# Where the norm, the scores and the inverse stand in the gaps of an RWKV-7 recurrence: a new order of the work beside the chain

## The chip, the core and the metric

The kernel runs on one core of a Trainium2 chip. A core has five engines that each work through a queue of their own, in its order: TensorE (PE in the profile; its weight loads are PEld), VectorE (DVE), ScalarE (ACT), GpSimd (POOL) and SyncE (SP), which here issues the transfers between the chip's memory and the core. An engine waits for another, or for a transfer, at a semaphore, and what stands behind the waiting instruction in its queue waits with it. The metric is the device time of one execution, in microseconds (us), as the median of several runs.

## What is computed

The reference is a decoder of two layers over 1040 tokens (16 meta tokens and 1024 of input) of width 1024, in float32: a layer of RWKV-7 time mixing, a layer of stick-breaking attention, each followed by a conv-gated MLP. The change lies in the time mixing. Cut to that part, with 16 heads of 64:

```python
kk = kk / jnp.maximum(jnp.linalg.norm(kk, axis=-1, keepdims=True), 1e-12)
decay = jnp.exp(-jnp.exp(heads(w_log)))
seq = tuple(jnp.moveaxis(t, 1, 0) for t in (rh, decay, kh, vh, -kk, kk * ah))
def step(S, inp):
    r_t, w_t, k_t, v_t, a_t, b_t = inp
    sa = jnp.einsum('bhij,bhj->bhi', S, a_t)
    S = (S * w_t[:, :, None, :] + sa[..., None] * b_t[:, :, None, :]
         + v_t[..., None] * k_t[:, :, None, :])
    return S, jnp.einsum('bhij,bhj->bhi', S, r_t)
_, y = lax.scan(step, S0, seq)
mu = jnp.mean(y, axis=-1, keepdims=True)
var = jnp.mean(jnp.square(y - mu), axis=-1, keepdims=True)
y = ((y - mu) * lax.rsqrt(var + GN_EPS)).reshape(bsz, L, C) * lnx_g + lnx_b
y = y + bonus                     # sum(r * k * r_k) * v
return (y * g) @ w_o
```

## The kernel before

The scan is done in chunks of 64 tokens (`rwkv_chain`). Within a chunk the steps become matrix products and the inverse of a triangular matrix; from chunk to chunk only the state S goes on. The first 16 tokens are a chunk of their own (`first_chunk`). The other 1024 tokens are two segments of 8 chunks, and the heads are four groups of four, so there are eight **units**, one for each segment and group, each with 8 chunks.

`stage_c` is the serial chain of a unit. For each chunk PE forms c1 (S against the scaled keys), DVE adds KV and writes R, PE forms c2 with the inverse XT, DVE and ACT copy the result into UV, PE forms c3 and the output yp, and DVE writes the next S. Three times in a chunk, behind c1, behind c2 and behind c3 and yp, it calls `gap()`, and there work for other units is put into the queues. A unit so has 24 gaps, gap 0 to gap 23; gaps 3k, 3k+1 and 3k+2 are those of chunk k.

What a gap gets stands in the table `SEQ`, one word for each gap, each letter one step of a generator. In unit i:

- A: a step of `stage_a` of unit i+2. It loads BK and AR (the load of AR goes into the tiles ARz), forms the scores between them on PE, masks them on DVE into Aa, and sends their diagonal blocks through memory into another layout (AD is written, AT is read back): the *lanes*. P is its first step, the load of BK, for unit i+3.
- S, s: a step of `stage_s`, the substitution that inverts the diagonal blocks, of unit i+2 (S) or i+1 (s). It copies XL from xinit on DVE, then does 62 tensor operations on POOL, a product into prd and a sum into XL in turn, each of which needs the one before. At the end XL is written to memory as XD. A unit's substitution is done partly under S, in the unit before, partly under s.
- x, X: a step of `stage_x` of unit i+1. The first (x) first runs what is left of that unit's substitution, and loads XD back as X11t. The second transposes X11t into X on DVE and copies it into XT on ACT (XTb in the trace). Six more finish the inverse on PE and ACT.
- B, V, T: masked scores against r (Ar), the turned v and its product KV, and the turned BK, all of unit i+1.
- F: a step of `stage_f` of unit i-1, the norm of its output y. Step 1 loads g into the tile GB. Step 2 squares y on ACT (ysq), multiplies y by g on POOL, and loads b into the same tile GB. Steps 3 and 4 are four products each on PE (hr_gn), 5 to 9 the reciprocal root on DVE and ACT, 10 and 11 two products each on PE (hp_gn) for one half of y. Step 12 multiplies this half on DVE and starts the other one, step 13 ends its products, and step 14 multiplies the second half on DVE, adds b to y on POOL and writes y out. In unit 0, F is the rest of `first_chunk`.

PE, DVE, POOL and SP keep the order in which the generators write (`InOrder`, `pmm`); on ACT the scheduler places most instructions. In the last unit, `beside` adds steps of the output projection from gap 13 on.

Of the kernel before, what the change touches and what calls it, by code (L numbers as in the profile page):

```python
# [51 lines left out]
def kernel(ctx: ExitStack, tc: tile.TileContext, a: dict, out: bass.AP):  # L52
# [729 lines left out]
    def rwkv_chain(late, early, last):  # L782
# [564 lines left out]
        def run(gs):  # L1347
# [8 lines left out]
        ).split()  # L1356
        NZ = (1, 4, 12)
        SEQ = (
            "ATsss TVsss TTsss AAsss AAsss AAsss AAsss Asss FBsss BBsss xFV BFV "
            "BFVS BFVSSS BFVSSS BFVSSS BFVSSS XVFSSS XFSSS XFSSS XFSSS XFSSS XFPSSS XFFSSSS "  # L1360
        ).split()

        def warm(n):
# [198 lines left out]
    def rest():  # L1562
# [300 lines left out]
        def chain_and_wo(es):  # L1863
# [40 lines left out]
            def last():  # L1904
# [9 lines left out]
                return work  # L1914

            run(rwkv_chain(*pools, last))
            late.close()
            rw.close()
# [620 lines left out]
```

## Time and profile before

| | us |
|---|---|
| median of 3 runs | 3629.34 (3625.01 to 3632.36) |
| the profiled execution | 3628.45 |
| its span, first to last instruction | 3626.7 |
| the eight units, first c1 to the end of the last chunk | 432.8 (754.85 to 1187.60) |
| mean granted clock of PE over the span, share of full | 0.911 |

The profile is one execution, and its times count from the first instruction. What lies outside the span is 1.75 us. The units are 12% of the span; the projections ahead of them and the second layer and MLPs behind them are not touched. The start of a unit is called U here, and U+10 is a point 10 us into it. In the timeline a row is start, duration, engine, line, operation and the tiles it writes and reads; the bracket at its end is the idle time of the engine before it, and what ended it. Several operations of one kind in a row are merged, and x4 counts them. The rows are further down, ahead of the prediction.

### The profile page before, as it was taken

The numbers are of one execution on the slowest core, as the hardware profiler recorded it, in microseconds if no ns is written. First come the engines' busy times: TensorE is split into PE (matmuls) and PEld (weight loads), VectorE is DVE, ScalarE is ACT, GpSimd is POOL, SyncE is SP. The second block draws the span as 40 slices with busy tenths as digits, with TensorE's granted clock in tenths as the row PEclk, the third lists the DMA queues.
The fourth block names the chain that finished last, engine by engine and source line by source line (L and its number), as shares of the span: only waits on it lengthen the run. The fifth ranks groups of instructions, "written<-read, shape, count | busy, mean of one in ns | idle before, by whom it ended". The sixth has DMA issues, their size and how long they took to land.

```text
span 3626.7 us, 62709 instructions
## 1 busy us (share of the span) xinstructions
PE 3120.0 (86%) x25101; PEld 2913.6 (80%) x25101; DVE 2329.0 (64%) x3128; ACT 1554.7 (43%) x2859; POOL 1735.9 (48%) x1678
## 2 busy tenths in 40 slices
PE   4798688567778979999899988888889699998998
PEld 4796466456667969999899978788878699998998
DVE  8778866523333588888733377777774988887342
ACT  4664545133335333333333266666654333334232
POOL 5555634344535564454422366666644544444231
PEclk7898799768777989999999999999999799999999
DMA  6344333433335422222445200110035222224453
GB/s 202 104 152 140 123 122 116 119 94 98 106 99 156 138 65 77 83 71 80 150 137 167 90 27 24 27 30 24 21 108 168 90 79 77 77 81 138 122 170 94
DMA packets 439454, 366.61 MB, mean 101 GB/s; under 512 B 66855, under 2 KB 359485, under 8 KB 438907
## 3 DMA queue, kind: packets, MB, share of 16 engines
q1 hardware_dynamic: 438299, 361.28, 33.0%
q8 instruction: 197, 3.23, 0.4%
q0 software_dynamic: 864, 1.33, 0.1%
q14 instruction: 94, 0.77, 0.1%
HBM read 266.51 MB, written 96.02 MB: 100 GB/s over the span
## 4 chain that ended last, share of the span: by engine, by line
PE 45%; DVE 20%; DMA 9%; ACT 6%; issue 5%; POOL 4%; SPq 2%; ACTq 0%; DVEq 0%; POOLq 0%
PE dn L1517 12%; DVE t L1700 5%; DVE om L2254 2%; PE kps L2099 2%; DVE rs L1625 2%; DMA AD<-Aa 2%; PE c L797 1%; POOL be L2257 1%; SPq L44 1%; ACT t L1698 1%; PE wt L2102 1%; PE kp L217 1%; DMA XD<-XL 1%; PE av L2099 1%; PE A L797 1%
## 5 line engine op out<-in xcount | busy, mean ns | idle before, releaser
L1517 PE MATMUL dn<-act,h_dn 128*128 128x260 f32 x2688 | 437.5, 284 | 4.8 <-ACT act L76 2.4
L1517 PEld LDWEIGHTS dn<-act,h_dn 128*128 128x128 f32 x2688 | 373.5, 190 | 5.8 <-ACT act L76 2.8
L1700 DVE SCALAR_TENSOR_TENSOR t<-u,pcol,t 128x1040 f32<-128x1040 f32 x168 | 303.4, 1806 | 108.9 <-ACT t L1698 108.9
L1517 PE MATMUL dn<-act,l_dn 128*128 128x260 f32 x1344 | 273.4, 285 | 1.7 <-POOL l_dn L1466 1.7
L2257 POOL TENSOR_TENSOR be<-be,om 128x911 f32<-128x911 f32 (+7 forms) x128 | 195.8, 1530 | 131.1 <-DVE om L2254 106.6
L1466 POOL TENSOR_TENSOR l_dn<-r_dn,h_dn 128x1024 fp32r<-128x1024 f32 (+1 forms) x46 | 102.5, 2228 | 323.5 <-ACT h_dn L76 322.8
L2254 DVE TENSOR_TENSOR_SCAN om<-om 128x912 f32<-128x912 f32 (+7 forms) x128 | 214.0, 1672 | 49.2 <-POOL om L2249 30.4
L1715 POOL TENSOR_TENSOR t<-t,t 128x1040 f32<-128x1040 f32 x42 | 102.5, 2440 | 253.4 <-DVE t L1700 253.4
L76 ACT ACTIVATE h_dn<-r_dn 128x1024 fp32r<-128x1024 f32 (+1 forms) x92 | 90.7, 986 | 298.2 <-PE dn L1517 276.7
L1517 PEld LDWEIGHTS dn<-act,l_dn 128*128 128x128 f32 x1344 | 207.3, 189 | 2.2 <-POOL l_dn L1466 2.2
L1466 POOL TENSOR_TENSOR s34l<-rs,s34h 128x1024 fp32r<-128x1024 f32 x44 | 105.8, 2404 | 101.1 <-ACT s34h L76 101.1
L76 ACT ACTIVATE WT<-wt 128x512 fp32r<-128x512 f32 (+2 forms) x224 | 98.8, 443 | 117.1 <-PE wt L2102 88.8
L797 PE MATMUL A<-ARz,BK 128*128 128x128 f32 x512 | 91.3, 326 | 58.9 <-DMA ARz<-AR_s 34.1
L2320 DVE TENSOR_TENSOR WT<-wt,WT 128x512 fp32r<-128x512 f32 (+2 forms) x224 | 107.6, 488 | 51.6 <-ACT WT L76 48.2
L2099 PE MATMUL av<-WT,VS 128*128 128x256 f32 (+3 forms) x640 | 108.7, 283 | 32.9 <-DVE WT L2320 32.7
L76 ACT ACTIVATE s34h<-rs 128x1024 fp32r<-128x1024 f32 x44 | 46.7, 1062 | 202.2 <-PE p110S L1652 5.0
L1466 DVE TENSOR_TENSOR l_dn<-r_dn,h_dn 128x1024 fp32r<-128x1024 f32 (+1 forms) x46 | 52.0, 1131 | 122.6 <-ACT h_dn L76 122.5
L2102 PE MATMUL wt<-ident,be 128*128 128x128 f32 x576 | 99.2, 295 | 33.6 <-DVE WTm L2295 33.5
L797 PEld LDWEIGHTS A<-ARz,BK 128*128 128x128 f32 x512 | 75.6, 224 | 65.2 <-issue 34.8
L217 PE MATMUL kp<-xm,wh_rw_wk 128*128 128x264 f32 (+1 forms) x384 | 109.0, 376 | 19.1 <-DVE xm L396 10.5
L2249 POOL TENSOR_SCALAR_AFFINE_SELECT be<-be 128x128 f32<-128x128 f32 x128 | 78.0, 610 | 90.0 <-ACT be L2244 90.0
L2099 PEld LDWEIGHTS av<-WT,VS 128*64 128x64 f32 (+1 forms) x640 | 85.5, 165 | 44.0 <-DVE WT L2320 42.9
(2105 smaller groups left out, 11090.1 us busy)
## 6 DMA issues: line engine op xcount, KB each, us to landing
r_dn<-in_ffn_down_dram SPq DMA_DIRECT2D x60, 512.0 KB
a_s<-t SPq DMA_DIRECT2D x84, 260.0 KB
rv<-in_ffn_up_dram SPq DMA_DIRECT2D x42, 512.0 KB
ra<-in_ffn_up_dram SPq DMA_DIRECT2D x42, 512.0 KB
araw<-a_s SPq DMA_DIRECT2D x50, 260.0 KB
r_dn<-in_ffn_down_dram SPq DMA_DIRECT2D x32, 384.0 KB
raw<-a_s SPq DMA_DIRECT2D x36, 260.0 KB
hr<-h_s SPq DMA_DIRECT2D x32, 260.0 KB
```

What stands on the lines that cost most here:

```text
L76: return S.activation(o, i, AF.Copy, scale=scale)
L217: return tc.keep_in_program_order(mm(*args, **kw))
L797: return tc.keep_in_program_order(mm(*args, **kw))
L1466: eng.tensor_tensor(lo, x, f(hi), op=ALU.subtract)
L1517: self.mm(ps[:, c, :], w[:, kk, :], X[k][i][:, c * CH : (c + 1) * CH], start=k == 0 and j == 0, stop=k == len(X) - 1 and j == 2,)
L1700: VV.scalar_tensor_tensor(t[j], u[j][:, i : i + n], w, t[j], op0=ALU.mult, op1=ALU.add)
L1715: (G if n == L else VV).tensor_tensor(t[1], t[0], t[1], op=ALU.mult)
L2099: return tc.keep_in_program_order(mm(*args, **kw))
L2102: return tc.keep_in_program_order(nc.tensor.transpose(*args))
L2254: V.tensor_tensor_scan(om[0:nq, 0:nk], om[0:nq, 0:nk], om[0:nq, 0:nk], 1.0, op0=ALU.mult, op1=ALU.min)
L2257: G.tensor_tensor(be[0:nq, 1:nk], be[0:nq, 1:nk], om[0:nq, 0 : nk - 1], op=ALU.mult)
L2320: V.tensor_tensor(wt[:, 1, s0:s1], ps[:, s0:s1], f(wt[:, 0, s0:s1]), op=ALU.subtract)
```

## The change

The table `SEQ` is written anew; nothing else differs.

```diff
         SEQ = (
-            "ATsss TVsss TTsss AAsss AAsss AAsss AAsss Asss FBsss BBsss xFV BFV "
-            "BFVS BFVSSS BFVSSS BFVSSS BFVSSS XVFSSS XFSSS XFSSS XFSSS XFSSS XFPSSS XFFSSSS "
+            "AFss TFs TVFs TFss TFs TFss AFs AAFss AAFs AAFs AAFss BVFs "
+            "BVFss BVFFss BVFsss BVFxS BVS BVSS BVXS BXSS XXS XSS XXSP XSSF "
         ).split()
```

F moves from gaps 8 to 23 into gaps 0 to 13: its step 1 from gap 8 to gap 0, its step 14 from gap 22 to gap 13. The matrix products of A move from gaps 3 to 6 into gaps 6 to 10, those of B from gaps 8 to 15 into gaps 11 to 18. The first step x moves from gap 10 to gap 15, the second, X, from gap 17 to gap 18. Of a unit's 62 substitution operations, 12 now stand in the unit before and 50 in the unit that ends them; it was 34 and 28.

On POOL, the multiplication of y by G stood behind the last operation of the substitution of unit i+1 (XL 128x16) and before the first one of unit i+2. In unit 2 before (s ends, F begins):

```order
L44 TENSOR_TENSOR XL_7395<-XL_7395,prd_7419 128x16x2
L44 TENSOR_TENSOR prd_7419<-AT_7169,XL_7395 128x16
L44 TENSOR_TENSOR XL_7395<-XL_7395,prd_7419 128x16
L44 TENSOR_TENSOR y_7085<-y_7085,G_7928 128x1024
L44 TENSOR_TENSOR prd_8066<-AT_7816,XL_8042 128x2x31
L44 TENSOR_TENSOR XL_8042<-XL_8042,prd_8066 128x2x31
```

In the same unit of the changed kernel, around the addition of B to y (the last step of F):

```order
L44 TENSOR_TENSOR prd_7499<-AT_7205,XL_7477 128x8x17
L44 TENSOR_TENSOR XL_7477<-XL_7477,prd_7499 128x8x17
L44 TENSOR_TENSOR prd_7499<-AT_7205,XL_7477 128x8x16
L44 TENSOR_TENSOR y_7063<-y_7063,B_7744 128x1024
L44 TENSOR_TENSOR XL_7477<-XL_7477,prd_7499 128x8x16
L44 TENSOR_TENSOR prd_7499<-AT_7205,XL_7477 128x10x15
```

Both operations on y now stand inside the substitution of unit i+1: the multiplication behind 14 of its 62 operations, the addition behind 31, ahead of the last 31.

On SP, the transfers of unit 2 before:

```order
L44 DMA BK_01_7698<-BK_s_125 128x1024
L44 DMA ARz_5797<-AR_s_117 64x1024 x4
L44 DMA vc_7768<-vc_s_132 128x2x512
L44 DMA AD_7815<-Aa_7814 32x8x32 x4
L44 DMA AT_7816<-AD_7815 128x1x1024
L44 DMA AD_7815<-Aa_7814 32x8x32 x4
L44 DMA AT_7816<-AD_7815 128x1x1024
L44 DMA G_7928<-g_s_138 128x2x512
L44 DMA XD_7953<-XL_7395 256x1x64 x4
L44 DMA X11t_7969<-XD_7953 32x8x64 x4
L44 DMA B_7978<-b_s_146 128x2x512
```

and of the same unit in the changed kernel:

```order
L44 DMA ARz_5797<-AR_s_117 64x1024 x4
L44 DMA G_7721<-g_s_138 128x2x512
L44 DMA B_7744<-b_s_146 128x2x512
L44 DMA vc_7769<-vc_s_132 128x2x512
L44 DMA AD_7851<-Aa_7850 32x8x32 x4
L44 DMA AT_7852<-AD_7851 128x1x1024
L44 DMA AD_7851<-Aa_7850 32x8x32 x4
L44 DMA AT_7852<-AD_7851 128x1x1024
L44 DMA y_s_93<-y_7063 128x512
L44 DMA y_s_95<-y_7063 128x512
L44 DMA XD_8113<-XL_7477 256x1x64 x4
L44 DMA X11t_8118<-XD_8113 32x8x64 x4
```

G and B are now loaded ahead of vc, and the two writes of y stand ahead of XD; before they came at the end of the unit, ahead of the next BK.

On DVE, unit 2 of the changed kernel from chunk 4 (Rz, the second half of y, UV, S) to the transposition X of chunk 6:

```order
L44 TENSOR_TENSOR Rz_5801<-c_7989,KV_7326 64x2x64 x2
L44 TENSOR_TENSOR Ar_7968<-A_7969,maskA 128x512
L44 TENSOR_TENSOR y_7063<-y_7063,hp_gn_7980 128x512
L44 COPY UV_7325<-c_8012 64x2x64
L44 SCALAR_TENSOR_TENSOR S_8062<-c_8036,PC,PS_7988 128x64 x2
L44 TENSOR_TENSOR Ar_7968<-A_8018,maskA 128x512
L44 COPY XL_8124<-xinit 128x512
L44 TENSOR_TENSOR Rz_5802<-c_8068,KV_7326 64x2x64 x2
L44 COPY UV_7325<-c_8130 64x2x64
L44 TENSOR_TENSOR Ar_7968<-A_8073,maskA 128x512
L44 SCALAR_TENSOR_TENSOR S_8180<-c_8151,PC,PS_8067 128x64 x2
L44 STREAM_TRANSPOSE X_8119<-X11t_8118 128x512
```

In the kernel before, X stood ahead of the second halves of y:

```order
L44 STREAM_TRANSPOSE X_7970<-X11t_7969 128x512
L44 SCALAR_TENSOR_TENSOR S_8192<-c_8160,PC,PS_8110 128x64 x2
L44 TENSOR_TENSOR Rz_5801<-c_8197,KV_7334 64x2x64 x2
L44 COPY UV_7333<-c_8229 64x2x64
L44 TENSOR_TENSOR y_7085<-y_7085,hp_gn_8219 128x512
L44 SCALAR_TENSOR_TENSOR S_8282<-c_8258,PC,PS_8196 128x64 x2
L44 TENSOR_TENSOR Rz_5802<-c_8287,KV_7334 64x2x64 x2
L44 TENSOR_TENSOR y_7085<-y_7085,hp_gn_8276 128x512
```

The two multiplications of y moved from chunks 6 and 7 to chunks 3 and 4, and X from the end of chunk 5 into chunk 6.

## Rows read from the trace of the kernel before

**Rows 1.** Windows by stretch: length, busy of PE, PEld, DVE, ACT, POOL, PEclk, DMA.

```profile
754.85:807.58 52.73, 39.79 (x615) 34.17 (x613) 17.97 (x57) 20.59 (x57) 19.17 (x53) 0.76 0.26 57
807.58:1101.38 293.80, 220.04 (x3204) 189.25 (x3201) 94.42 (x290) 109.42 (x290) 137.88 (x316) 0.77 0.38 100
860.15:921.00 60.85, 43.83 (x645) 37.70 (x641) 18.89 (x58) 21.99 (x58) 27.98 (x65) 0.75 0.40 101
1101.38:1140.90 39.52, 35.98 (x611) 30.27 (x609) 16.00 (x53) 21.80 (x58) 17.01 (x38) 0.87 0.30 88
1140.90:1187.60 46.70, 36.28 (x413) 31.14 (x414) 17.56 (x51) 20.53 (x50) 21.74 (x15) 0.74 0.80 245
909.76:921.00 11.24, 11.24 (x182) 9.86 (x181) 3.35 (x10) 4.50 (x12) 7.67 (x14) 0.50 0.01 1
1133.82:1140.90 7.08, 6.81 (x181) 5.83 (x181) 3.29 (x10) 5.10 (x15) 1.30 (x1) 1.00 0.01 2
```

**Rows 2.** Waits of the eight units: waiter, releaser: total us, times, longest.

```profile
DVE X L44 <- DMA X11t<-XD: 58.0, 6, 11.5
...
PE A L797 <- DMA ARz<-AR_s: 24.3, 4, 7.3
```

**Rows 3.** Timeline of SP, unit 2: issue, time it took.

```profile
861.21 0.94 SPq L44 DMA_DIRECT2D BK<-BK_s  x2
862.25 2.46 SPq L44 DMA_DIRECT2D ARz<-AR_s  x4
...
890.57 0.55 SPq L44 DMA_DIRECT2D AT<-AD  x1
...
891.77 4.48 SPq L44 DMA_DIRECT2D XD<-XL  x4
902.40 1.79 SPq L44 DMA_DIRECT2D X11t<-XD  x4
```

**Rows 4.** Timeline of PE, units 1 and 2.

```profile
826.94 0.45 PE L797 MATMUL c<-S,ARz 128*64 128x64 f32 x8
...
872.67 2.05 PE L797 MATMUL A<-ARz,BK 128*128 128x128 f32 x8 [7.31 <-DMA ARz<-AR_s]
```

**Rows 5.** Timeline of POOL, units 2 and 3: the substitution and the two operations on y.

```profile
866.02 0.40 POOL L44 TENSOR_TENSOR prd<-AT,XL 128x120 f32<-128x120 f32 x1
...
875.97 0.25 POOL L44 TENSOR_TENSOR XL<-XL,prd 128x16 f32<-128x16 f32 x1
901.75 2.34 POOL L44 TENSOR_TENSOR y<-y,G 128x1024 f32<-128x1024 f32 x1 [25.54 <-DMA G<-g_s]
...
909.73 0.35 POOL L44 TENSOR_TENSOR prd<-AT,XL 128x96 f32<-128x96 f32 x1
...
913.64 0.40 POOL L44 TENSOR_TENSOR prd<-AT,XL 128x120 f32<-128x120 f32 x1
...
918.82 2.35 POOL L44 TENSOR_TENSOR y<-y,B 128x1024 f32<-128x1024 f32 x1 [2.63 <-DVE y L44]
...
923.16 0.46 POOL L44 TENSOR_TENSOR XL<-XL,prd 128x128 f32<-128x128 f32 x1
...
936.80 0.25 POOL L44 TENSOR_TENSOR XL<-XL,prd 128x16 f32<-128x16 f32 x1
```

**Rows 6.** Timeline of DVE, unit 2: the wait for X, and the operations behind it.

```profile
905.78 0.71 DVE L44 STREAM_TRANSPOSE X<-X11t 128x512 f32<-128x512 f32 x1 [9.23 <-DMA X11t<-XD]
...
907.72 0.61 DVE L44 TENSOR_TENSOR Rz<-c,KV 64x128 f32<-64x128 f32 x2 [0.88 <-PE c L797]
...
918.05 0.69 DVE L44 TENSOR_TENSOR y<-y,hp_gn 128x512 f32<-128x512 f32 x1 [1.53 <-PE hp_gn L797]
```

**Rows 7.** Timeline of SP, unit 6, where no lanes are made.

```profile
1117.47 2.52 SPq L44 DMA_DIRECT2D XD<-XL  x4
1121.59 2.38 SPq L44 DMA_DIRECT2D X11t<-XD  x4
```

**Rows 8.** Timeline of PE, unit 6: products of one step of F (hp_gn), full clock.

```profile
1134.82 0.71 PE L797 MATMUL hp_gn<-ident,ysq 128*128 128x128 f32 x4
```

## The prediction

> **What bounds the kernel now.** The change touches only the eight units of the recurrence, so I read the windows cut at their borders first. Units 1 to 5 take 293.8 us together, 58.8 each. Unit 6, in which no scores are made and no lanes go through memory, takes 39.5, and unit 7 takes 46.7 [rows 1]. What stage C does in unit 6 is the same as in unit 2 (60.85). So about 20 us of a unit are not the serial chain but waits, and the list of waits names two. DVE waits for X11t six times, 58.0 us in all, and PE four times for ARz, 24.3 in all [rows 2]. Behind the first the clock is low as well: in unit 2 the stretch from c2 of chunk 6 to the next unit has a granted clock of 0.50 (1.2 GHz) and takes 11.24; the same stretch of unit 6, which had no such wait, has 1.00 (2.4 GHz) and takes 7.08 [rows 1].
>
> Where they come from is read off the timelines of unit 2 (U = 860.15). ARz is issued at 862.25 behind BK, and its first reader, a product of A in gap 3, stands on PE until 872.67 [rows 3, 4]. X comes late for another reason: POOL had ended the substitution at 876.22, U+16, but XD was issued at 891.77, because SP stood in order behind the second AT, which waited for AD until 890.57 [rows 3, 5]. X11t was then issued at 902.40 and X began at 905.78 after 9.23 idle [rows 3, 6]. POOL is no bound: it idles 25.54 for G [rows 5]. In the kernel before, X is late by SP's order, not by POOL's.
>
> **Part 1, scores later.** A's first product moves from gap 3 to gap 6. BK and ARz, 2 MB, took from 861.21 to 872.67, 11.5 us [rows 3, 4]. BK no longer stands behind the writes of y, which now come in mid-unit, so only ARz's 1 MB is left at U and should land by about U+7 (half of 11.5, and a little for its later issue); gap 6 comes at about U+9. I take the wait of 24.3 as gone. It is covered by six gaps of other work; without them it would be back.
>
> **Part 2, the norm first.** F's steps cost PE what they cost before, in other gaps. What counts is where its two POOL operations now stand: the addition of B is ahead of the last 31 operations of unit i+1's substitution, and it needs the second half of y from DVE, F's step 14, in gap 13. Before, nothing of F stood ahead of the end of the substitution. So a new path runs through each unit that has a next one, in five pieces.
>
> (a) From U to the second half of y. Unit 1 has no wait for ARz; from U = 807.58 to chunk 4 it took 19.4 [rows 1, 4]. Moved in are three pairs of products of hp, 0.71 each, and one more step of hr, taken as large as one of hp: 2.8. Moved out are three steps of B of two products each; the record of four such products is 2.05 at 1.2 GHz, so 0.5 a step at full clock: 1.5 [rows 4, 8]. On DVE the masks of A now stand ahead of S in chunk 2 and of UV in chunk 3, each waiting for products that a later gap issues; an operation of that size takes 0.69 [rows 6]: 1.4 more. Chunk 4's first gap then holds 1.7 us of PE work (hp, B, V) and y itself 0.69. Sum 19.4 + 2.8 - 1.5 + 1.4 + 2.4 = 24.5. Ends: 21.5, if the chain's own waits hide the additions, and 27.5, if V waits for vc (below).
>
> (b) The addition of B takes 2.35 [rows 5].
>
> (c) The last 31 operations on POOL, XL 128x128 to XL 128x16, ran from 923.16 to 937.05: 13.9 [rows 5]. Each needs the one before, so nothing shortens this. POOL gets to the addition in time: the multiplication by G starts once G has landed behind ARz, about U+9; it takes 2.34, and the 17 operations behind it run at 0.49 each (eight from 909.73 to 913.64), 8.3 in all [rows 5]. That is U+20, ahead of U+24.5.
>
> (d) XD to X. With nothing else in the queue, XD to X11t took 4.1 (1117.47 to 1121.59) [rows 7], and X11t to X 3.4 (902.40 to 905.78) [rows 3, 6]. SP has the lanes 14 us behind it by then. Sum 7.5.
>
> (e) X to the next unit. X now stands ahead of Rz of chunk 6: 0.71, then Rz 0.61 [rows 6], then the stretch that took 11.24 at 1.2 GHz [rows 1]. F's three pairs of hp are out of it, up to 1.4 each at this clock (twice 0.71, rows 8's price) [rows 8], but a step of X fills the place of one; I take 2.0 off, between nothing and 3.5. Sum 10.5.
>
> A unit is then 24.5 + 2.35 + 13.9 + 7.5 + 10.5 = 58.8, with (a) and (e) giving 55 to 62. DVE would reach X at about U+34 and waits until U+48: a wait of some 14 us instead of 9, which gives back what ARz saves.
>
> A rule of the Trainium skill bears on (c). The row first: a product of 128x120 takes 0.40 on POOL both at 866.02 and, with DVE's operations on y and S around it, at 913.64 [rows 5], so the trace shows no slowing. The Trainium skill (GPSIMD Engine Reference, section 1, Specifications) says that GpSimd shares its SBUF interfaces with VectorE, with contention when a DVE instruction has two SBUF inputs. By the row (c) stays 13.9; were it a tenth slower by the rule, six units would add 8 us.
>
> **The sum.** Units 1 to 5: 5 x 58.8 = 294.0 against 293.8, so nothing. Unit 6 loses its freedom: it has no lanes, but it has F and the substitution for unit 7, and before the substitution ended there at 1117.4, U+16, with an empty queue [rows 7]. Now it goes through the same path. Without A's products (a) is some 2.5 shorter, 22.0: 56.3 against 39.5, so +16.8. Unit 0 has the small F of the first chunk: its addition comes in gap 9 and leaves 29 operations behind it. It waits for X before and after; taken as unchanged, within 4 either way. Unit 7 has F earlier and the output projection from gap 13, also unchanged within 4. Outside the units nothing moves. The profiled execution of 3628.45 (span 3626.7), 0.9 under the median of 3629.34, becomes 3628.45 + 17 = 3645.5.
>
> **Rivals.** First, on the other side: the clock returns sooner. If PE ran at 2.4 GHz from X on in all six units, (e) would lose 3.4 (the ratio 7.08 to 11.24 on the 9.2 left) and the start of the next unit some 1.5: about 5 a unit, 30 in all, 3615.5, faster. It is faster than before from some 17 us on, 3 of these 5 a unit. For it: unit 6 shows the short stretch [rows 1]. Against: there no wait came first, and after the wait in unit 2 the clock was 0.50 to the end of the unit, and the new wait is longer. Chance 0.06.
>
> Second, the clock returns later. Behind X PE has fewer products than before, since hp is gone, and gap 0 has none. If 1.2 GHz lasts through gaps 0 to 5, where I count three gaps, that is 1.5 a unit, 9 in all, 3654.5. The Trainium skill (TensorE: Matmul & The Clock Gate, section What's actually happening) puts it as the throttled state being the default, which activity releases; that points the same way, and 0.50 behind the wait agrees [rows 1]. Chance 0.12.
>
> Third, SP. The load of B now waits for POOL's multiplication by G, as both use the tile GB, and vc stands behind it on SP. If vc lands after gap 11, V's products hold PE, and (a) is up to 3 longer in units 1 to 5: 15 us, 3660.5. B issued at U+11.5 with vc lands at some U+18 (1 MB, half of 11.5, and the issue), and gap 11 comes at U+18 to U+19, so it is close. Chance 0.12.
>
> Fourth, the additions to the first four chunks hide in PE's idle time, and (a) is 21.5 in all six units: 18 less, 3627.5, the same as before. For it: PE is busy 44 of 61 us in unit 2 [rows 1]. Against: most of the idle time is the two waits. Chance 0.14.
>
> **How the numbers follow.** My forecast, 3636 to 3655, has 0.56. Slower than 3628.45 by over 0.2% (7.3 us, about what a measurement of this kernel tells from none) are the forecast, the second and the third: 0.80. Within it is the fourth: 0.14. Faster is the first: 0.06. The range takes the fourth in at its low end and the third at its high end: 3626 to 3662. The ends of (e) and of units 0 and 7 lie inside.
>
> **What would show it.** PE's wait for ARz is gone, and the first product of A stands in U+9 to U+11. DVE's wait for X11t comes in seven units, 0 to 6, with 12 to 16 us in units 1 to 6. POOL's addition of B waits for DVE's y until about U+24.5, and the last XL of a unit ends at U+41, not U+16; XD goes out right behind it. Unit 6 takes 56, not 39.5. The forecast fails if the last XL ends before U+37 (then (a) is short), or if X begins more than 8 behind it (then (d) is long, and the loss larger), or if unit 6 stays near 40.

## The result and the profile after

The changed kernel takes 3663.59 us (median of 4 runs, 3659.55 to 3667.32) against 3629.07 for the kernel before (4 runs); the ratio is 1.0094, with a 95% interval of 1.0078 to 1.0110. It is slower by 34.5 us, where the prediction said 17 and its range ended at 3662. The profiled execution takes 3661.98, with a span of 3660.3. One of the four runs of the last experiment (e10) was in a slower state, 3930.62 us at a granted clock of 0.722, and its figures are those of the other three.

First the windows of the changed kernel, which answer to [rows 1]: unit 0, units 1 to 5, unit 2 alone, unit 6, unit 7 to the start of its last chunk, and all behind that; then the start of unit 1 (to gap 5), the start of unit 2 (to gap 5), and in unit 2 the stretch from c2 of chunk 6 to the next unit.

```profile
core 0: us, PE busy (x) PEld busy (x) DVE busy (x) ACT busy (x) POOL busy (x), PEclk, DMA share, GB/s
754.23:807.02 52.79, 39.01 (x614) 33.39 (x613) 17.68 (x57) 20.56 (x57) 21.08 (x56) 0.76 0.25 67
807.02:1114.57 307.55, 213.11 (x3203) 186.41 (x3201) 96.92 (x290) 112.07 (x290) 141.08 (x320) 0.75 0.36 98
867.00:930.29 63.29, 44.67 (x642) 39.19 (x641) 19.35 (x58) 22.44 (x58) 28.18 (x64) 0.72 0.35 97
1114.57:1170.27 55.70, 36.78 (x611) 31.84 (x609) 16.44 (x53) 22.33 (x58) 23.43 (x51) 0.75 0.22 68
1170.27:1209.74 39.47, 30.51 (x363) 26.42 (x361) 17.42 (x46) 19.13 (x45) 20.66 (x14) 0.69 0.84 262
1209.74:3660.30 2450.56, 2245.16 (x17068) 2189.38 (x17068) 1653.91 (x1862) 1033.88 (x1812) 1158.91 (x939) 0.95 0.29 89
807.02:816.02 9.00, 8.21 (x92) 7.10 (x89) 2.28 (x9) 4.55 (x11) 0.00 (x0) 0.72 0.70 177
867.00:879.11 12.11, 11.32 (x90) 9.90 (x88) 2.28 (x9) 4.69 (x11) 3.12 (x4) 0.50 0.49 131
920.78:930.29 9.51, 9.14 (x200) 8.17 (x201) 2.67 (x9) 4.71 (x12) 0.00 (x0) 0.50 0.17 65
```

And of the kernel before the two windows that [rows 1] does not have, unit 7 to the start of its last chunk and all behind it:

```profile
1140.90:1182.12 41.22, 30.80 (x357) 26.36 (x357) 14.99 (x45) 20.18 (x48) 19.42 (x14) 0.75 0.85 263
1182.12:3626.70 2444.58, 2235.10 (x17073) 2178.94 (x17072) 1653.98 (x1863) 1033.98 (x1810) 1160.51 (x940) 0.96 0.29 89
```

Read together, the 33.6 by which the span grew are: units 1 to 5 +13.75, unit 6 +16.18, the stretch behind the units +5.98, unit 7 -1.75, unit 0 and the start -0.6. Unit 6 is what the prediction said it would be (56.3, measured 55.70). Units 1 to 5 should have stayed equal and did not.

The list of waits in the units (waiter, releaser: total, times, longest), to be held against [rows 2]:

```profile
DVE X L44 <- DMA X11t<-XD: 117.2, 7, 17.7
PE c L797 <- DVE Rz L44: 116.4, 25, 16.3
```

The wait of PE for ARz is no longer in the list. The wait for X has doubled, and all of it reaches PE. Where it comes from stands on POOL in unit 2 (U = 867.00): the multiplication by G, the addition of B, and the first and the last of the operations behind it.

```profile
875.83 2.35 POOL L44 TENSOR_TENSOR y<-y,G 128x1024 f32<-128x1024 f32 x1 [21.78 <-DMA G<-g_s]
...
895.32 2.35 POOL L44 TENSOR_TENSOR y<-y,B 128x1024 f32<-128x1024 f32 x1 [8.67 <-DVE y L44]
897.63 0.46 POOL L44 TENSOR_TENSOR XL<-XL,prd 128x128 f32<-128x128 f32 x1
...
911.47 0.24 POOL L44 TENSOR_TENSOR XL<-XL,prd 128x16 f32<-128x16 f32 x1
```

on SP, which has the lanes behind it by then,

```profile
899.27 0.57 SPq L44 DMA_DIRECT2D AT<-AD  x1
899.95 0.89 SPq L44 DMA_DIRECT2D y_s<-y  x2
911.74 2.56 SPq L44 DMA_DIRECT2D XD<-XL  x4
915.93 1.80 SPq L44 DMA_DIRECT2D X11t<-XD  x4
```

and on DVE:

```profile
894.55 0.69 DVE L44 TENSOR_TENSOR y<-y,hp_gn 128x512 f32<-128x512 f32 x1 [0.18 <-PE hp_gn L797]
...
919.43 0.71 DVE L44 STREAM_TRANSPOSE X<-X11t 128x512 f32<-128x512 f32 x1 [17.29 <-DMA X11t<-XD]
```

POOL stands idle for 21.78 and again for 8.67, the first time with 48 operations of the substitution queued behind what it waits for, the second time with 31. In the kernel before it had ended the same substitution at U+16 [rows 5]; now the last XL ends at U+44.7 in unit 2, and XD goes out at once.

### The profile page after: what moved, and what is told of

The parts are those of the page before. It is cut to its first block, busy times and chain, and to the rows that moved or that the text cites. A ratio compares the mean times of both kernels' runs of the same rounds, so it can differ in the third digit from the quotient of the medians.

```text
span 3660.3 us, 62706 instructions
## 1 busy us (share of the span) xinstructions
PE 3121.7 (85%) x25101; PEld 2921.8 (80%) x25101; DVE 2334.4 (64%) x3128; ACT 1556.2 (43%) x2859; POOL 1738.0 (47%) x1678
## 4 chain that ended last, share of the span: by engine, by line
PE 47%; DVE 20%; POOL 6%; ACT 6%; issue 5%; DMA 5%; SPq 1%; ACTq 0%; DVEq 0%; POOLq 0%
PE dn L1517 12%; DVE t L1700 5%; DVE om L2254 2%; PE kps L2099 2%; DVE rs L1625 2%; PE c L797 2%; PE wt L2102 1%; ACT t L1698 1%; PE kp L217 1%; PE av L2099 1%; PE wo L1517 1%; PE wo L1909 1%; POOL be L2257 1%; PE vps L2099 1%; PE A L797 1%
## 5 line engine op out<-in xcount | busy, mean ns | idle before, releaser
L797 PE MATMUL c<-Rz,XTb 128*64 128x64 f32 x256 | 34.5, 272 | 116.6 <-DVE Rz L44 116.4
L2102 PE MATMUL wt<-ident,be 128*128 128x128 f32 x576 | 100.0, 297 | 33.6 <-DVE WTm L2295 33.5
L797 PEld LDWEIGHTS c<-Rz,XTb 128*64 128x64 f32 x256 | 25.0, 171 | 124.0 <-issue 113.3
L217 PE MATMUL kp<-xm,wh_rw_wk 128*128 128x264 f32 (+1 forms) x384 | 107.0, 372 | 18.8 <-DVE xm L396 10.5
```

Of the source, the lines that this page charges most:

```text
L217: return tc.keep_in_program_order(mm(*args, **kw))
L797: return tc.keep_in_program_order(mm(*args, **kw))
L2102: return tc.keep_in_program_order(nc.tensor.transpose(*args))
```

## The experiments

Ten kernels were run. Each was timed beside the kernel before on its own chip; the units are those of the profiled run, which lies up to 11 us from its kernel's median (e4: 3650.03).

| kernel | median us | ratio to before, 95% interval | units 1 to 5 | unit 6 |
|---|---|---|---|---|
| before | 3629 | 1 | 293.8 | 39.5 |
| changed | 3663.59 | 1.0094 (1.0078 to 1.0110) | 307.6 | 55.7 |
| e1, B behind the substitution | 3620.20 | 0.9979 (0.9968 to 0.9991) | 270.8 | 46.2 |
| e2, G and B behind it | 3605.72 | 0.9943 (0.9924 to 0.9963) | 268.2 | 51.6 |
| e3, before, scores later alone | 3642.72 | 1.0050 (1.0032 to 1.0068) | 299.8 | 37.7 |
| e4, before, x earlier alone | 3638.83 | 1.0034 (1.0015 to 1.0054) | 312.8 | 42.1 |
| e5, x between the two AT | 3610.63 | 0.9939 (0.9919 to 0.9959) | 274.3 | 52.7 |
| e6, PE kept at work in the wait | 3672.89 | 1.0102 (1.0072 to 1.0132) | 309.4 | 61.9 |
| e7, scores back | 3666.17 | 1.0085 (1.0058 to 1.0112) | 314.6 | 60.6 |
| e8, three lessons in one order | 3605.36 | 0.9923 (0.9903 to 0.9943) | 265.7 | 46.0 |
| e9, small products at the unit's border | 3686.38 | 1.0152 (1.0124 to 1.0181) | 320.0 | 59.1 |
| e10, e8 with the second AT later | 3588.40 | 0.9875 (0.9851 to 0.9898) | 242.7 | 47.8 |

In e2 and e5 unit 0, which the table leaves out, is shorter too: 41.5 us instead of 52.8 in the changed kernel.

### Is it the addition of B on POOL? (e1)

The changed kernel with F's last step behind x:

```diff
-            "BVFss BVFFss BVFsss BVFxS BVS BVSS ...
+            "BVFss BVss BVsss BVxFFFS BVS BVSS ...
```

> The changed kernel, with F's step 14 (second half of y on DVE, addition of B on POOL, writes of y) moved from gap 13 to gap 15, behind x and so behind the end of the substitution. All else stays. Theory 1 (the addition of B on POOL holds the last 31 operations, and through them X): POOL goes from the multiplication by G (ends about U+11) straight through 48 operations, 8.3 + 14.0 = 22.3 us, so the last XL ends at about U+33.5 instead of U+41 to U+45; X follows 7.7 later and the next unit 10.9 behind that: units 1 to 5 take about 52 each instead of 61.5, unit 6 47 to 50 instead of 55.7. Sum 50 to 55 off: about 3610 us. Theory 2 (the units are long because PE's clock comes back late and its gaps are fuller): nothing of that is changed, the time stays at 3655 to 3665.

Measured 3620.20, some 42 below the changed kernel (0.9979 against 1.0094 of the kernel before). Units 1 to 5 take 54.2 each, unit 6 46.2. POOL and DVE of e1 in unit 2 (U = 869.9):

```profile
878.75 2.35 POOL L44 TENSOR_TENSOR y<-y,G 128x1024 f32<-128x1024 f32 x1 [18.16 <-PE c2b L797]
...
903.43 0.24 POOL L44 TENSOR_TENSOR XL<-XL,prd 128x16 f32<-128x16 f32 x1
903.63 2.34 POOL L44 TENSOR_TENSOR y<-y,B 128x1024 f32<-128x1024 f32 x1
```

```profile
913.42 0.71 DVE L44 STREAM_TRANSPOSE X<-X11t 128x512 f32<-128x512 f32 x1 [11.14 <-DMA X11t<-XD]
```

The last XL ends at U+33.8 (33.5 expected) and X begins at U+43.5 instead of U+52.4. Moving this one step, the addition with its operation on DVE and its writes of y, takes back more than the whole loss; on POOL the 31 operations no longer stand behind a wait for y. Theory 2 falls.

### Both operations behind (e2)

Of the edit, the lines that are added at the end of the norm:

```diff
+            if glate:
+                G.tensor_tensor(y, y, G1, op=ALU.mult)
+                B1 = B1()
             G.tensor_tensor(y, y, B1, op=ALU.add)
```

In units 1 to 6 the two are left out where they stood; x goes into gap 9 and F's last step into gap 15.

> The changed kernel, with both of F's operations on POOL (times G, plus B, with the load of B between them) behind the end of the substitution in units 1 to 6, F's step 14 in gap 15, and x pulled in gap 9 so that XD and X11t stand on SP between the first AT and the second AD. Theory 1: nothing stands ahead of the substitution, its last XL ends at about U+23.5, X11t is there at U+31, ahead of the place where DVE comes to X (about U+34), so the wait of DVE for X11t is gone from units 1 to 6, and a unit takes 44 to 48: 85 to 90 off 363 for units 1 to 6, about 3577 us (3560 to 3595), faster than the kernel before. Theory 2 (late clock, fuller gaps): units stay above 56 and the time above 3635.

Measured 3605.72, faster than before, but only two thirds of what was expected. The wait for X is down to 35.1, and another stands in its place: POOL waits for B, 99.5 us in six times, because B can be loaded only behind the multiplication by G. So y is written late, and BK and ARz of the next unit stand behind those writes on SP (U = 852.5 here):

```profile
857.18 0.82 SPq L44 DMA_DIRECT2D y_s<-y  x2
858.05 0.93 SPq L44 DMA_DIRECT2D BK<-BK_s  x2
859.03 2.47 SPq L44 DMA_DIRECT2D ARz<-AR_s  x4
```

ARz is issued at U+6.6, and the first product of A waits 4.0 although it stands in gap 6. This is the wait of the kernel before, come back.

### What the first part is worth (e7, e3)

The changed kernel with the scores back in gaps 3 to 6:

```diff
-            "AFss TFs TVFs TFss TFs TFss AFs AAFss AAFs AAFs AAFss BVFs "
+            "AFss TFs TVFs AATFss AATFs AATFss AAFs AFss Fs Fs Fss BVFs "
```

> The changed kernel with its first part undone: A's products again from gap 3 on, the norm still first. Theory 1 (part 1 takes a wait for ARz away that the new order has hardly any more, since the writes of y and BK no longer stand ahead of ARz on SP): ARz is issued at about U and lands at U+7 to U+8, the first product comes at U+6 to U+7, so a wait of 0 to 2 a unit, and the second half of y is later by as much: 3660 to 3675 us. Rival (part 1 is worth the 24.3 that the wait cost before, once nothing hides it): about 3688 us.

Measured 3666.17: no difference from the changed kernel that these runs can tell, and no wait for ARz in the list; in unit 2 ARz is issued at 867.29 (U = 867.6) and the first product of A stands at U+7.2. With the norm first, y is written in mid-unit, ARz leaves SP at U, and F's steps make the first three gaps long enough. So beside the second part of the change the first is worth nothing that these runs show.

The kernel before with the scores later and nothing else:

```diff
-            "ATsss TVsss TTsss AAsss AAsss AAsss AAsss Asss FBsss BBsss xFV BFV "
+            "ATsss TVsss TTsss sss sss sss Asss AAsss AAFBsss AABBsss AAxFV BFV "
```

> The kernel before, with A's products alone moved from gaps 3 to 7 into gaps 6 to 10 (the first part of the change). Theory 1: PE's wait for ARz (24.3) is gone, but X11t still stands on SP behind the second AT, which comes no sooner, so DVE's wait for X11t grows from 58 to about 80 and gives it back: 3624 to 3634 us. Rival: the wait for ARz is a loss of its own, and its removal brings 20 to 25: about 3606 us.

Measured 3642.72, 0.5% slower: both expectations missed, the rival by more. ARz comes no sooner (the first product stands at U+12.6, as before), the gaps ahead of it are now empty and pass at full clock, so gap 6 comes at U+8.6 and a wait is left, 3.99 in unit 2 (U = 866.75; the profile names no releaser for this one):

```profile
879.35 1.19 PE L797 MATMUL A<-ARz,BK 128*128 128x128 f32 x4 [3.99 <-issue]
```

The rest of the products stand on top of the norm's in gaps 7 to 10, and the wait for X stays (61.8).

### Is X, late by SP's order, a loss of its own? (e4)

The kernel before with x in gap 6:

```diff
-            "ATsss TVsss TTsss AAsss AAsss AAsss AAsss Asss FBsss BBsss xFV BFV "
+            "ATsss TVsss TTsss AAsss AAsss AAsss AAxsss Asss FBsss BBsss FV BFV "
```

> The kernel before, with x alone pulled from gap 10 into gap 6, so that XD and X11t stand on SP ahead of the second AD and AT. The norm and the scores stay where they were. Theory 1 (in the kernel before X is late by SP's order): POOL ends the substitution at U+16, X11t is issued by about U+26 instead of U+42, DVE's wait for X11t (58.0) is gone, and as no wait comes ahead of the last stretch of a unit, its clock stays high there: units 1 to 5 take 45 to 49 instead of 58.8, 50 to 70 off: about 3570 us. Rival (POOL or the lanes set X, and SP's order is a sham): 3620 to 3630 us.

Measured 3638.83, 0.3% slower, outside both expectations. The wait for X is gone, 6.3 instead of 58.0, so it was SP's order that made X late; but nothing is gained. The list of waits of e4:

```profile
PE A L797 <- DMA ARz<-AR_s: 52.5, 5, 12.3
DVE y L44 <- POOL y L44: 51.0, 5, 11.3
...
DVE X L44 <- DMA X11t<-XD: 6.3, 1, 6.3
```

SP in unit 2 (U = 865.1) shows why:

```profile
889.92 0.57 SPq L44 DMA_DIRECT2D AT<-AD  x1
890.58 3.14 SPq L44 DMA_DIRECT2D XD<-XL  x4
900.55 1.79 SPq L44 DMA_DIRECT2D X11t<-XD  x4
902.39 1.94 SPq L44 DMA_DIRECT2D AD<-Aa  x4
905.65 0.56 SPq L44 DMA_DIRECT2D AT<-AD  x1
906.26 0.58 SPq L44 DMA_DIRECT2D G<-g_s  x1
```

G stands behind the second AT and leaves at U+41 (in the kernel before at U+31, between the AT and the XD of [rows 3]). DVE waits for the multiplication by G, y is written late, and BK and ARz of the next unit, behind it, are late as well (ARz is issued at U+8.5 in unit 3, U+2.1 in unit 2 of the kernel before): the wait for ARz doubles. In the kernel before the norm was nearly as late as X (in unit 2 the multiplication by G ended at U+43.9 and X began at U+45.6), and the wait for X hid it.

### Is it the clock? (e6, e9)

The changed kernel with products that nothing uses, first 60 in gap 18, inside the wait:

```diff
-            ... BVS BVSS BVXS BXSS XXS XSS XXSP XSSF "
+            ... BVS BVSS BVXSW BXSS XXS XSS XXSP XSSF "
```

> The changed kernel, with 60 products of the identity with itself on PE in gap 18, in the time in which PE waits for X (units 0 to 6). They add work that nothing uses. Theory clock (what follows the wait runs at 1.2 GHz because PE idled in the wait, and this costs): the 10.86 from X to the next unit becomes 7.1 to 8.5, and the late starts of units 2 and 5 (3.4 each) are gone; X itself stays where it is. 20 to 30 off: about 3638 us, if the products fit into the wait of 16 (60 at 0.18 to 0.3 are 11 to 18). Rival (the clock has no part in the loss, all is X's arrival): 3655 to 3670.

Measured 3672.89, 1.0102 against 1.0094: no gain, and just above the rival's range. The windows of unit 2 are the wait, the stretch from c2 of chunk 6 to the next unit, and the next unit's gaps 0 to 5:

```profile
908.22:926.31 18.09, 15.30 (x152) 14.88 (x149) 1.29 (x4) 2.63 (x5) 11.61 (x35) 1.00 0.33 84
926.31:935.70 9.39, 9.02 (x200) 8.05 (x201) 2.65 (x9) 4.71 (x12) 0.00 (x0) 0.51 0.17 65
935.70:947.83 12.13, 11.34 (x93) 9.92 (x89) 2.28 (x9) 4.69 (x11) 3.04 (x3) 0.50 0.51 131
```

The wait is filled but for a rest at its end, and the clock is 1.00 in it; in the next stretch it is 0.51 all the same. In unit 2 PE idles 2.80, from 923.51 to its first product behind the wait,

```profile
926.31 0.24 PE L797 MATMUL c<-Rz,XTb 128*64 128x64 f32 x1 [2.80 <-DVE Rz L44]
```

and the granted clock falls to 0.50 at 926.50. In units 1 to 6 the rest is 2.8 to 3.6, and the clock falls 0.2 to 2.0 behind it; in unit 0 no idle time there is longer than 1.0, and the clock falls 0.3 behind the last one. So e6 does not tell the idle time from the work that follows it: only unit 0 speaks against the idle time. In the changed kernel the clock falls within the wait itself, in unit 2 at 907.70, 2.8 into an idle time of 15.88, as the prediction read it [rows 1].

Then four such products at the end of each of gaps 19 to 23, 0 and 1:

```diff
-            "AFss TFs ... BXSS XXS XSS XXSP XSSF "
+            "AFssW TFsW ... BXSSW XXSW XSSW XXSPW XSSFW "
```

> The changed kernel, with four products of the identity with itself (some 0.9 us at 2.4 GHz) at the end of each of the gaps 19 to 23 and 0 and 1, in units 0 to 6, work that nothing uses. Theory (the clock falls behind X and comes back late at the next unit's start because the chain alone, without F's products, keeps PE too little busy, and not because PE idled in the wait for X): the stretch from X to the next unit has a clock well above 0.50, gaps 2 and 3 are at 1.00 in all units, so that no unit has the 3.4 of units 2 and 5 more than another. The products themselves cost up to 0.5 a gap, so the time is 3645 to 3665: little net, but the units are even. Rival (the clock has nothing to do with it): 0.50 from X on as before, units as uneven, and the products cost 3 to 5 a unit: 3680 to 3700 us.

Measured 3686.38, slower than the theory's 3645 to 3665, in the rival's range; but the profile is the theory's. The windows of e9 are unit 2 from U to gap 5, its stretch from c2 of chunk 6 to the next unit, and from U to gap 18:

```profile
878.13:887.65 9.52, 9.25 (x129) 8.31 (x129) 2.75 (x11) 4.52 (x13) 1.45 (x1) 1.00 0.67 167
927.85:940.99 13.14, 13.14 (x240) 11.80 (x241) 2.68 (x9) 5.63 (x14) 0.00 (x0) 0.80 0.13 48
878.13:910.30 32.17, 30.32 (x430) 26.64 (x429) 15.32 (x46) 14.03 (x41) 16.73 (x30) 1.00 0.46 125
```

The clock still falls in the wait, but it comes back within the stretch, in unit 2 5.3 behind the end of the wait (927.85 to 933.16) instead of 14.2 in the changed kernel (920.78 to 935.00). Over units 1 to 5 it takes 5.1 to 13.4 from the end of the wait in e9, against 14.2 to 23.6 in the changed kernel. Chunk 0 takes 5.58 in each of units 1 to 6, where the changed kernel takes 6.05 to 7.23; the late starts of units 2 and 5 are gone. The products cost more than that gives back: the last stretch is 13.14 instead of 9.51. More work of PE behind the wait so brings the clock back sooner, the late clock was real, and nothing is won by work without use.

### What else sets X (e5, e8, e10)

In the changed kernel, 17 more operations ahead of the multiplication by G, and x between the two AT (it leaves gap 15):

```diff
-            "AFss TFs TVFs TFss TFs TFss ... AAFs AAFs AAFss BVFs "
+            "AFsssssssssssssssss TFs TVF TF TFs TFss ... AAFs xAAFs AAFss BVFs "
```

> The changed kernel, with F's steps in their gaps, but 17 more substitution operations ahead of the multiplication by G on POOL (in gap 0), so that they fill the time in which G is on its way, and x in gap 9, between the first AT and the second AD on SP. The addition of B then stands behind the whole substitution. Theory 1 (what POOL does ahead of the last XL, and what SP holds ahead of XD, set X): 17 operations take 8.3 from U, the multiplication 2.3, the other 31 13.9: the last XL ends at about U+25, X11t is there at U+33, when DVE comes to X (U+34 to U+36), so the wait for X is gone or under 2. Unlike in the run with both operations behind, B is loaded early, so the writes of y and ARz of the next unit are not late. A unit takes 42 to 46: some 90 off 363 for units 1 to 6, about 3570 us. If something else on SP or in the norm still comes late (as with x earlier in the kernel before), the units stay at 50 and the time at 3595 to 3605.

Measured 3610.63, a little above the second of the two expectations. The next unit's first operations on POOL wait until 859.08, U+4.0 (U = 855.1); the second AT was issued at 847.01, behind X11t, and the list of waits gives AT as the releaser three times (75.3) and the writes of y behind it on SP three times (62.2). So the multiplication by G begins at 872.32, U+17, and B and vc stand behind it on SP; the turning of vc on PE then waits:

```profile
881.14 1.06 PE L800 MATMUL vt<-ident,vc 128*64 128x128 f32 x4 [4.00 <-DMA vc<-vc_s]
```

Then the scores early (as in e7), 14 operations in gap 0, and x behind the second AT:

```diff
+            "AFssssssssssssss TFs TVFs AATFs AATFs AATFss AAFs AFss Fs Fs Fss BVxF "
+            "BVF BVFF BVF BVFS BVS BVSS BVXS BXSS XXS XSS XXSP XSSF "
```

> The changed kernel with three of the runs' lessons in one order: A's products from gap 3 on again (so that both AT go out early), 14 substitution operations in gap 0 ahead of the multiplication by G (12 more than now), and x in gap 11, behind the second AT and ahead of F's last step. The last XL then ends at about U+26, XD goes out behind the second AT at about U+29, X11t is there at about U+37 and X comes 1 to 4 late; B, vc, the writes of y and BK stand where nothing waits for them. Expected: units of 46 to 50 instead of 60 to 64, 75 to 90 off: about 3580 us. If a late transfer or the lanes (AT into the next substitution) take the place of the wait again, as in the two runs with x between the ATs, the units stay at 52 to 54 and the time near 3605.

Measured 3605.36, the second of the two expectations; units 1 to 5 at 53.1, unit 6 at 46.0. The last XL of unit 2 ends at 888.65, yet X begins at 904.20. SP of e8:

```profile
889.95 0.56 SPq L44 DMA_DIRECT2D AT<-AD  x1
890.55 2.55 SPq L44 DMA_DIRECT2D XD<-XL  x4
900.68 1.79 SPq L44 DMA_DIRECT2D X11t<-XD  x4
```

From XD to X11t it takes 10.1. In the changed kernel it took 4.2 (911.74 to 915.93), in the kernel before 10.6 in unit 2 [rows 3] and 4.1 in unit 6 [rows 7], in e4 10.0. Over the units of all these kernels but e3, where the second AD and AT stand between the two, it is 8.2 to 11.7 where a load of AT was issued up to 1.5 ahead of XD (in the kernel before one of G too), and 4.1 to 5.8 where it was issued 5.5 or more ahead. So the last run issues the second AT behind X11t, with one more step of A in gap 12 for it (the lines of the edit are shortened here):

```diff
                 LQ.dma_start(AD...)
+                if u:
+                    yield
                 LQ.dma_start(AT...)
```

> As the run with the three lessons in one order (e8), with one change: the load of the second AT (0.5 MB, spread over all partitions) is issued behind X11t instead of ahead of XD. In e8 the last XL ended at U+27.7 and XD went out at U+29.6, but X11t could be issued only 10.1 later, where the same step took 4.1 with an empty queue; theory: the packets of AT stand ahead of those of XD in the DMA engines. Then XD goes out at U+27.7, X11t at U+32, X at U+35.5, when DVE comes to it, and units 1 to 5 take 44 to 47 instead of 53: 30 to 40 off e8, about 3570 us. Against it: AT lands some 10 later, at U+44 or so, and the first 12 operations of the next substitution start that much later; if this holds G's multiplication or the last XL of the next unit, the units stay at 50 or more and the time above 3590.

Measured 3588.40, ratio 0.9875 (0.9851 to 0.9898): 1.25% faster than the kernel before by this ratio, and the best of all. SP and DVE of e10 in unit 2 (U = 853.9):

```profile
883.28 2.55 SPq L44 DMA_DIRECT2D XD<-XL  x4
888.05 1.79 SPq L44 DMA_DIRECT2D X11t<-XD  x4
889.88 0.56 SPq L44 DMA_DIRECT2D AT<-AD  x1
```

```profile
891.41 0.71 DVE L44 STREAM_TRANSPOSE X<-X11t 128x512 f32<-128x512 f32 x1 [6.00 <-DMA X11t<-XD]
```

XD to X11t is 4.8, and units 1 to 5 take 48.5. That is above the 44 to 47 expected, and the counterpart named there shows: POOL's next substitution now waits for AT (45.3 in three times). The Trainium skill (DMA: Bandwidth & Descriptors, section Queues, rings and completion order) says that each DMA engine takes descriptors in ring order; the 10 against 4 agree with it, as XD came behind AT in the same queue. No run here tells this order from two transfers that share the memory's rate.

## Where the prediction was wrong, and where it was right

The time lies outside the range of 3626 to 3662. The step that failed is term (a), from U to the second half of y: 24.5 forecast for units 1 to 5, 26.4 measured in the mean. It was added up from unit 1 of the kernel before, in which the granted clock was at 0.50 (1.2 GHz) for the first 3.6 us; in the changed kernel it was there for the first 4.7 to 6.2 in units 1, 3, 4 and 6, and for 13.4 and 14.1 in units 2 and 5. Unit 1 before, and unit 2 of the changed kernel:

```profile
807.58:811.21 3.63, 3.63 (x33) 2.73 (x32) 0.86 (x3) 2.38 (x5) 3.08 (x8) 0.50 0.88 226
867.00:880.39 13.39, 12.60 (x114) 11.18 (x112) 2.74 (x11) 5.43 (x13) 4.25 (x6) 0.50 0.50 133
```

Why the clock came back so much later in just these two units is not shown. A second term, the stretch outside the units, was put at nothing and came out at 5.98, without a cause that a run shows.

The direction and the mechanism were right: the addition of B stands ahead of the last 31 operations, X comes through it, and the wait for X swallows what ARz gives back. e1 shows it. The pieces, as the prediction named them:

- **Part 1.** The wait for ARz is gone, but e7 shows that the norm's new place does this by itself. The prediction had given the credit to the six gaps of cover, and expected the wait back without them. e7 contradicts this: its wait for ARz was nil.
- **(a), U to the second half of y.** Forecast 24.5 for units 1 to 5, 22.0 for unit 6. The second half ended at U+24.9, 28.2, 24.8, 25.4 and 28.5 in units 1 to 5, 9.3 more in sum, and 20.9 in unit 6. In units 1, 3 and 4 the count holds to 1. In units 2 and 5 the clock was still at 0.50 in gaps 2 to 4 (in unit 2 U to gap 5 takes 12.11, against 9.00 in unit 1), and in unit 2 both steps of F's hr took 1.75 instead of the 0.98 of unit 1: 3.4 a unit. This is the second rival, in two units of five instead of a little in each. In e9 the clock is up from U and the second half ends at U+24.2 in each of units 1 to 5.
- **(b), (c), (d), (e).** Forecast 2.35, 13.9, 7.5 and 10.5; measured 2.35, 14.04, 7.7 to 8.1 and 10.86 in units 1 to 5, the same in each to 0.01 but for (d). Together 0.9 a unit, 4.4 in five. In the changed kernel DVE was at work for only 2.8 of the 14.1 us of the 31 operations in unit 2, so this says little of a POOL slowed by DVE. In unit 2 of e8 (874.69 to 888.65) it was at work for 8.29 of their 13.96, and they took no longer. So the slower POOL that the prediction weighed by the Trainium skill (GPSIMD Engine Reference, section 1, Specifications) did not show here; how many of these DVE instructions had two SBUF inputs was not counted.
- **Unit 6**: 55.70 against 56.3.
- **Units 0 and 7**: +0.1 and -1.75, inside the 4 that each was given.
- **The signs**: seven waits for X came, XD went out right behind the last XL, and unit 6 was long. But the waits in units 1 to 6 were 17.1 to 17.7 instead of 12 to 16, the first product of A stood at U+13.9 in unit 2 (U+10.6 in unit 1) instead of U+9 to U+11, and the last XL ended at U+44.7 and U+44.9 in units 2 and 5 instead of U+41. The late XL and the late product are the clock of units 2 and 5; the waits are longer by it in units 2 and 5, and in the others because DVE came to the place of X sooner than U+34 (U+31.7 in unit 3).
- **Outside the units**, where nothing was to move: the stretch behind the last chunk took 2444.58 before and 2450.56 after. Its code is the same. In e1 it took 2452.09 and in e5 2446.35, so such differences come and go between profiled runs with one code; the kernel before stands at the low end. The 5.98 are not an effect that a run ties to the change, and what makes them was not settled.

So of the 17 that were missed, some 7 are the clock at the start of units 2 and 5, 7 are small sizes in (a) to (e), and the rest lies in a stretch that no edit touches, less the 1.75 of unit 7. The first rival (the clock returns sooner) did not happen. The third (vc late) did not either: B was issued at U+11.2 and vc 0.6 behind it, and no wait for vc is in the list; e5, where the multiplication by G came 8 later, shows that wait and its size. The fourth (the additions to (a) hide) fell.

One reading was only half of it: that the low clock behind X came from the wait for X. The row for unit 6 with 1.00 had two things that unit 2 lacked, no wait and a stretch with F's products at full clock [rows 1, 8]. In the changed kernel the clock does fall in the wait. But e9 leaves the wait and adds products behind it, and the clock comes back sooner, some 9 us in unit 2. Whether the clock would fall without the wait is open: e6 takes most of the idle time away, but the 2.8 to 3.6 that are left in units 1 to 6 end just ahead of the fall. The Trainium skill (TensorE: Matmul & The Clock Gate, section What's actually happening) calls the throttled clock the default, which activity releases; the sooner return in e9 agrees, but PE counted as busy for 9.02 of 9.39 behind the wait in e6 and was granted 0.51.

And the prediction called the waits for ARz and X "20 us of a unit" that are not the chain. e3 and e4 show that neither could be had alone: behind each stood other waits that took its place.

## What to carry to other kernels

An operation that is moved on an in-order engine holds all that is queued behind it: list for each engine, POOL and SP too, what then stands behind the moved instruction and who ends its chain, and put the operation that waits behind the long serial run, not into it (e1: one step of the norm, 42 us). A wait removed is worth only the distance to the next one: before a wait is counted as a gain, look for what else becomes ready at the same time (e3, e4). Where one queue carries all transfers, the small ones on the critical path go ahead of the bulky ones (e10).

## What the runs showed of the hardware

- A load of AT (0.5 MB in all 128 partitions, read from memory) just ahead in the queue made the step from XD to X11t 8.9 to 10.1 in units 1 to 5 of e8, instead of 4.2 to 4.8 in e10, where that load is issued behind it.
- In unit 2 of e6 PE had 2.4 GHz through a filled wait, idled 2.80, and fell to 1.2 GHz (926.50) 0.2 behind that idle time; it had 1.2 GHz to the end of the unit though it counted as busy for 9.02 of the 9.39. In the changed kernel 1.2 GHz lasted for 14.2 from the end of the wait in unit 2, in e9, with four products more in each gap, for 5.3.
- A window that no edit touches, some 2450 us long, differed by up to 7.5 us between profiled runs (2444.58 in the kernel before, 2452.09 in e1).
